# A decoder step's start: bands and first blocks loaded first, the sample later, stores from ScalarE's queue

## The chip, the cores and the metric

The kernel runs on one core of a Trainium2 chip. The metric is the device time of one execution in microseconds, given as the median of the timed runs. TensorE multiplies, VectorE (DVE) and ScalarE (ACT) prepare its operands and take its results, and SyncE (SP) issues nearly all DMA transfers. [...]

## What is computed

One step of a two-layer decoder for 1024 prompt tokens and 64 sample tokens of width 1024, in float32. The change touches only the first mixer, which pools each token's normalised vector over the last 2, 4, 8 or 16 tokens, by group of channels, and the product that the first layer's gate will later need.

```python
# layer 0
u = rmsnorm(h, norm_mix[0])
for g, w in enumerate((2, 4, 8, 16)):            # four groups of 256 channels
    d[g] = (sum of the last w tokens of u[g]) / min(pos + 1, w) - u[g]
h += pool_scale * concat(d[g] @ pool_w[g])       # the sample has 15 earlier tokens in state_pool
h += relu(rmsnorm(h) @ w_up)**2 @ w_down
h += sigmoid(rmsnorm(h) @ w_ple_gate) * (p[0] @ w_ple_proj)
# layer 1 (latent attention, MLP, gate) and the final norm follow
```

## The kernel before

The stream `h` is kept transposed, channels on partitions, in three chunks of tokens (`CH`): chunks 0 and 1 hold 384 prompt tokens each, chunk 2 the last 256 prompt tokens and the 64 of the sample. A product in float32 accuracy is three matmuls on a split into a high and a low part (`mm3`, L188 to L190); the split is a cast on ScalarE (`split`, L146) and a subtraction on VectorE (L147), or the same with a scale (`split_scaled`, L150 and L151).

`pool_phase` is the first stage. The sums over a window are matmuls of a block of 128 tokens (`block_in`: load, sum of squares on ScalarE at L394, reciprocal root in eleven tiny VectorE steps, split into a `slab`) with a banded matrix that `bands` loads and casts (L434, L435). `diff` (L468) makes chunk c, half of its channels, from blocks 3c to 3c+2 and the one before; `diff_sample` (L480) makes the sample's from block 8 (`sample_in`: the sample's own tokens, normalised) and block 9 (`state_in`). `mix` multiplies by `pool_w` and adds to `h`, which `residual` has loaded by then. Until `residual` needs it, the memory of `h` serves as staging for what comes in: `stage(i)` gives place i of eight, 5 to 7 in chunk 0, 0 to 2 in chunk 1, 3 and 4 in chunk 2. There are five slabs and three `raw` tiles.

`proj` is work that nothing here waits for: the product of p[0] with `w_proj` for the gate far behind. 24 of these are spread over the stage to keep TensorE at work; `filler` adds them from the list `fill`. Each needs its chunk's p (`load_p`) and a half of `w_proj` (pieces `proj0_0` and `proj0_1`), is copied out of PSUM into one of three `t` tiles (L366) and stored to DRAM (L367).

The string `order` fixes the order in which this work is written: p loads p of a chunk, f adds so many fillers, b takes a block in (b8 is the sample), s the state, g the bands, d makes sums (chunk, half), S the sample's, m mixes (chunk, half), r loads the residual of a chunk, l writes the last rows. `Plan` loads a weight piece when a step needs it, and ahead of that, up to four pieces, after each step that allows it (`ahead`). What is written is a priority and not a strict order: a later instruction is put earlier on its engine where an earlier one is estimated not to be ready.

Of the kernel before, what the change touches and what calls it, by code (L numbers as in the profile page):

```python
# [24 lines left out]
NS = 64  # L25
T = SEQ + NS
NB = 8
TS = 8
# [3 lines left out]
BUF = 15  # L32
# [80 lines left out]
def kernel(ctx: ExitStack, tc: tile.TileContext, io: dict):  # L113
    nc = tc.nc
# [28 lines left out]
    pp_d = [dpool.tile([KT, P, n], F32, name=f"pp_d{c}") for c, (_, n) in enumerate(CH)]  # L143

    def split(hi, lo, x):
        nc.scalar.copy(out=hi, in_=x)  # L146
        nc.vector.tensor_tensor(out=lo, in0=x, in1=hi.bitcast(F32), op=ALU.subtract)  # L147

    def split_scaled(hi, lo, x, g):
        nc.scalar.activation(hi, x, AF.Copy, scale=g)  # L150
        nc.vector.scalar_tensor_tensor(  # L151
            out=lo, in0=x, scalar=g, in1=hi.bitcast(F32), op0=ALU.mult, op1=ALU.subtract)
# [27 lines left out]
    plan = Plan(load_piece)  # L180

    def raw_tile():
        return wpool.tile([P, 1024], F32, tag="raw", bufs=3, name="raw")
# [8 lines left out]
    S = {}  # L192
# [17 lines left out]
    def bank():  # L210
        return S["ps"].tile([P, 512], F32, tag="mm", bufs=8, name="mm")
# [7 lines left out]
    def slab():  # L219
        return S["hid"].tile([P, 2176], F32R, tag="hid", bufs=5, name="hid")  # L220

    def tmp(n):
        return S["tmp"].tile([P, 384], F32, tag="t", bufs=3, name="t")[:, :n]
# [4 lines left out]
    def tiny(tag, like):  # L228
        p, m = like
        return S["tmp"].tile([P, 10], F32, tag=tag, bufs=4, name=tag)[:p, :m]  # L230

    def rsqrt(v):

        y, t = tiny("y", v.shape), tiny("yt", v.shape)
        nc.vector.tensor_scalar(
            out=y.bitcast(I32), in0=v.bitcast(I32), scalar1=-0.5, scalar2=RSQRT_GUESS, op0=ALU.mult, op1=ALU.add)
        for _ in range(3):
            nc.vector.tensor_tensor(out=t, in0=y, in1=y, op=ALU.mult)
            nc.vector.scalar_tensor_tensor(out=t, in0=t, scalar=-0.5, in1=v, op0=ALU.mult, op1=ALU.mult)
            nc.vector.scalar_tensor_tensor(out=y, in0=t, scalar=1.5, in1=y, op0=ALU.add, op1=ALU.mult)  # L240
        return y
# [35 lines left out]
    def mean_eps(ss, dim):  # L277
        nc.vector.tensor_scalar(out=ss, in0=ss, scalar1=1.0 / dim, scalar2=EPS, op0=ALU.mult, op1=ALU.add)
        return ss
# [38 lines left out]
    def lin(c, w, k, m, mo, src=None):  # L318
        n = CH[c][1]
        wh, wl = (x.rearrange("p (k m) -> p k m", k=k) for x in w)  # L320
        ps = bank()[:, :n]
        x = src or U[c]
        mm3(ps, [(wh[:, i, mo:mo + m], wl[:, i, mo:mo + m], x[i][0], x[i][1]) for i in range(k)])
        return ps

    def four(w, nt):

        return [x[:, 256 * (nt % 4):256 * (nt % 4) + 256] for x in w]
# [5 lines left out]
    def pool_phase():  # L334
# [7 lines left out]
        blocks = {}  # L342
        WAIT, PAIRS = [], ((1, 2), (5, 4), (7, 6))

        pj = [plan.piece(f"proj0_{i}", io["w_proj"][0, i], parts=2 - i) for i in range(2)]
# [16 lines left out]
        def proj(nt, c, w):  # L362
            n = CH[c][1]
            ps = lin(c, four(w, nt), 2, P, 0, PP[c])
            t = tmp(n)
            nc.scalar.copy(out=t, in_=ps)  # L366
            nc.sync.dma_start(out=pp_d[c][nt], in_=t)  # L367

        def start():
            linear_open("1")  # L370
# [8 lines left out]
        def stage(i):  # L379

            c, i = (1, i) if i < 3 else (2, i - 3) if i < 5 else (0, i - 5)
            return h[c].rearrange("p k n -> p (k n)")[:, i * 1024:(i + 1) * 1024]

        def block_in(j):


            if not WAIT:
                E["bss"] = tiny("bss", (P, 2 if any(j == p[0] for p in PAIRS) else 1))
            i = len(WAIT)
            s = slab()  # L390
            blocks[j] = (s[:, 0:1024], s[:, 1024:2048])
            x = stage((3, 4, 0, 1, 2, 0, 3, 4)[j])
            nc.sync.dma_start(out=x, in_=io["x_prompt"][j * P:(j + 1) * P, :])
            nc.scalar.activation(blocks[j][0], x, AF.Square, accum_out=E["bss"][:, i:i + 1])  # L394
            WAIT.append((j, x))
            if any(j == p[0] for p in PAIRS):
                return
            g = rsqrt(mean_eps(E["bss"], D))
            for i, (j, x) in enumerate(WAIT):
                split_scaled(*blocks[j], x, g[:, i:i + 1])  # L400
                if j == 7:
                    E["g7"] = S["tmp"].tile([P, 1], F32, tag="g7", bufs=1, name="g7")
                    nc.vector.tensor_copy(out=E["g7"], in_=g[:, i:i + 1])
            WAIT.clear()

        def sample_in():
            ss = tiny("bss", (NS, 1))
            x, gb = stage(2)[0:NS], stage(7)[0:NS]
            nc.sync.dma_start(out=x, in_=io["x_sample"])
            nc.sync.dma_start(out=gb, in_=io["g_mix0"].partition_broadcast(NS))  # L410
            sq = raw_tile()[0:NS]
            nc.scalar.activation(sq, x, AF.Square, accum_out=ss)
            g = rsqrt(mean_eps(ss, D))
            nc.vector.scalar_tensor_tensor(out=x, in0=x, scalar=g, in1=gb, op0=ALU.mult, op1=ALU.mult)
            blocks[8] = x
            nc.sync.dma_start(out=io["pool_new"], in_=x)

        def last_rows():
            x, gb = raw_tile()[96:P], raw_tile()[96:P]
            nc.sync.dma_start(out=x, in_=io["x_prompt"][SEQ - 32:SEQ, :])  # L420
            nc.sync.dma_start(out=gb, in_=io["g_mix0"].partition_broadcast(32))
            nc.vector.scalar_tensor_tensor(out=x, in0=x, scalar=E["g7"][96:P], in1=gb, op0=ALU.mult, op1=ALU.mult)
            nc.sync.dma_start(out=io["pool_prompt"], in_=x[32 - BUF:32, :])

        def state_in():
            blocks[9] = stage(1)[0:NB * BUF]
            nc.sync.dma_start(out=blocks[9], in_=io["state"].rearrange("b t d -> (b t) d"))
            nc.sync.dma_start(out=io["pool_old"], in_=io["state"][:, TS:BUF, :])

        def bands():  # L430
            s = slab()
# [5 lines left out]
        def d_tile(c, dt):  # L437
            if (c, dt) not in E:
                E[c, dt] = u_pair(c)
            return E[c, dt]  # L440
# [30 lines left out]

        def diff_sample(x):
            xh = x[0].bitcast(F32).rearrange("p (g n) -> p g n", g=4)
            for dt in range(KT):
                g = dt // 2
                cs = slice(dt * P, (dt + 1) * P)
                ps = bank()[:, :NS]
                for bj, o in ((8, 16), (9, 16 + NS)):
                    b = blocks[bj]
                    nc.tensor.matmul(  # L480
                        out=ps, lhsT=b[:, cs], rhs=xh[0:b.shape[0], g, o:o + NS], start=bj == 8, stop=bj == 9)
                uh, ul = d_tile(2, dt)
                split(uh[:, 256:320], ul[:, 256:320], ps)

        def mix(c, gp, w):
# [3 lines left out]
            for gg in range(2):  # L489
# [8 lines left out]
                        op0=ALU.mult, op1=ALU.add)  # L498
                    touch(c, dt)

        fill = [(half, c, nt) for half, c in ((0, 2), (1, 2), (0, 0), (0, 1), (1, 0), (1, 1))
                for nt in range(4 * half, 4 * half + 4)]

        def filler(k):
            for half, c, nt in fill[:k]:
                plan.add(lambda w, nt=nt, c=c: proj(nt, c, w), pj[half])
            del fill[:k]

        def diffs(c, half):
# [2 lines left out]
        def mixes(c, gp):  # L512
# [2 lines left out]
                next_norm(c, gain("norm_mlp0"))  # L515

        order = (
            "p2 f1 b8 f3 b0 s f2 g p0 b1 f2 S b2 f1 b3 f2 p1 b5 d00 f2 d01 f2 b4 r0 "
            "b7 f1 r1 f1 m00 m01 f1 d10 d11 f2 b6 f1 m10 m11 f1 d20 f4 r2 d21 f1 m20 f1 m21 l").split()
        plan.add(start, ahead=False)  # L520
        for i, t in enumerate(order):
            k, a = t[0], int(t[1:] or 0)
            ah = i > 2
            if k == "p":
                plan.add(lambda a=a: load_p(a), ahead=ah)
            elif k == "l":
                plan.add(last_rows)
            elif k == "s":
                plan.add(state_in, ahead=ah)
            elif k == "b":  # L530
                plan.add(sample_in if a == 8 else lambda a=a: block_in(a), ahead=ah)
            elif k == "g":
                plan.add(bands, ahead=ah)
            elif k == "S":
                plan.add(diff_sample, gx)
            elif k == "f":
                filler(a)
            elif k == "d":
                diffs(a // 10, a % 10)
            elif k == "m":  # L540
                mixes(a // 10, a % 10)
            elif k == "r":
                plan.add(lambda a=a: residual(a))
# [875 lines left out]
```

## Time and profile before

| | us |
|---|---|
| median of 3 runs | 2416.49 |
| lowest and highest run | 2413.78, 2417.46 |
| the profiled execution, its own time | 2413.58 |
| its span in the trace | 2411.8 |
| TensorE busy in the span | 2361.0 (98%) |
| VectorE busy | 1226.1 (51%) |
| ScalarE busy | 829.4 (34%) |

The span is the time from the first to the last instruction that the profiler saw; the execution's own time is 1.8 us longer. Busy shares are means over a kernel whose stages differ, so the share of 98% says only that TensorE is the engine to look at, and where it isn't busy is read from the stretches.

### The profile page before, as it was taken

The page shows a single profiled execution, that of the slowest core. Times are in us where ns is not written, and L with a number is a line of the kernel's source. Part 1 is how long each engine was busy: PE and PEld are TensorE (multiplying, and loading weights), DVE is VectorE, ACT ScalarE, POOL GpSimd, SP SyncE. Part 2 cuts the span into 40 slices and gives each one's busy share as a digit, 9 for nine tenths or more (in the row PEclk, how much of TensorE's full clock was granted, in tenths as well). Part 3 has the DMA queues.
Part 4 walks back from the last instruction along what each step waited for, and adds up shares of the span by engine and source line. Part 5 has one row for each costly group of instructions (what it writes and reads, how often), then busy time and mean ns, then how long its engine had stood idle before and what let it go on. Part 6 is the DMA issues. An engine that isn't in the chain of part 4 may idle for free.

```text
span 2411.8 us, 35848 instructions
## 1 busy us (share of the span) xinstructions
PE 2361.0 (98%) x14516; PEld 2308.6 (96%) x14516; DVE 1226.1 (51%) x2406; ACT 829.4 (34%) x1557; POOL 11.0 (0%) x16
## 2 busy tenths in 40 slices
PE   7999999999999999998999999999999999999996
PEld 7999999999999999987988899999999999999996
DVE  5933333333333578477887765433333333334755
ACT  6622121121221444236777644312212212123432
POOL 0000000000000000000000000000000000000001
PEclk8999999999999999999999999999999999999998
DMA  8411111111111143257443351111111111111202
GB/s 269 125 55 44 44 45 44 44 44 47 49 47 44 40 124 130 58 153 223 149 126 125 94 200 55 52 47 49 44 44 44 44 44 44 44 44 44 64 27 78
DMA packets 97085, 186.53 MB, mean 77 GB/s; under 512 B 18633, under 2 KB 69001, under 8 KB 96144
## 3 DMA queue, kind: packets, MB, share of 16 engines
q1 hardware_dynamic: 90535, 179.78, 23.9%
q10 hardware_dynamic: 6384, 4.47, 0.6%
q8 instruction: 114, 1.87, 0.3%
q14 instruction: 52, 0.42, 0.1%
HBM read 155.00 MB, written 28.85 MB: 76 GB/s over the span
## 4 chain that ended last, share of the span: by engine, by line
PE 89%; DVE 4%; DMA 3%; ACT 2%; issue 1%; SPq 1%; ACTq 0%; DVEq 0%
PE mm L188 27%; PE mm L190 27%; PE mm L189 27%; PE s L891 2%; PE one L941 1%; PE one L1006 1%; PE one L918 1%; DMA craw<-in_cache 1%; PE mm L468 1%; ACT p L899 0%; PE mm L269 0%; DVE mx L898 0%; DVE hid L781 0%; PE one L188 0%; DMA hid<-row 0%
## 5 line engine op out<-in xcount | busy, mean ns | idle before, releaser
L188 PE MATMUL mm<-uh,whi 128*128 128x384 f32 (+1 forms) x2460 | 806.8, 328 | 12.8 <-ACT whi L146 5.9
L190 PE MATMUL mm<-uh,wlo 128*128 128x384 f32 (+1 forms) x2460 | 804.9, 327 | 0.2 <-DVE wlo L147 0.2
L189 PE MATMUL mm<-ul,whi 128*128 128x384 f32 (+1 forms) x2460 | 804.6, 327 | 0.0
L190 PE MATMUL mm<-hid,wlo 128*128 128x384 f32 (+1 forms) x1584 | 517.3, 327 | 0.0
L188 PE MATMUL mm<-hid,whi 128*128 128x384 f32 (+1 forms) x1584 | 517.1, 326 | 0.0
L189 PE MATMUL mm<-hid,whi 128*128 128x384 f32 (+1 forms) x1584 | 516.7, 326 | 0.0
L188 PEld LDWEIGHTS mm<-uh,whi 128*128 128x128 f32 x2460 | 464.0, 189 | 21.7 <-ACT whi L146 6.1
L190 PEld LDWEIGHTS mm<-uh,wlo 128*128 128x128 f32 x2460 | 463.9, 189 | 0.7 <-DVE wlo L147 0.7
L189 PEld LDWEIGHTS mm<-ul,whi 128*128 128x128 f32 x2460 | 464.0, 189 | 0.3 <-DVE ul L147 0.3
L146 ACT CAST whi<-raw 128x1024 fp32r<-128x1024 f32 (+3 forms) x184 | 190.9, 1038 | 753.1 <-PE mm L189 740.3
L314 DVE TENSOR_TENSOR h<-h,mm 128x384 f32<-128x384 f32 (+1 forms) x408 | 216.3, 531 | 422.2 <-PE mm L190 418.3
L188 PEld LDWEIGHTS mm<-hid,whi 128*128 128x128 f32 x1584 | 297.3, 188 | 3.8 <-issue 3.8
L190 PEld LDWEIGHTS mm<-hid,wlo 128*128 128x128 f32 x1584 | 297.3, 188 | 0.0
L189 PEld LDWEIGHTS mm<-hid,whi 128*128 128x128 f32 x1584 | 297.2, 188 | 0.0
L147 DVE TENSOR_TENSOR wlo<-raw,whi 128x1024 fp32r<-128x1024 f32 (+3 forms) x184 | 222.0, 1207 | 78.1 <-ACT whi L146 78.0
L557 DVE SCALAR_TENSOR_TENSOR t<-mm,r 128x384 f32<-128x384 f32 (+1 forms) x192 | 102.6, 535 | 299.4 <-PE mm L190 299.4
L559 ACT ACTIVATE t<-t 128x384 f32<-128x384 f32 (+1 forms) x192 | 97.0, 505 | 390.0 <-DVE t L557 390.0
L147 DVE TENSOR_TENSOR hid<-t,hid 128x384 fp32r<-128x384 f32 (+1 forms) x192 | 102.4, 534 | 140.4 <-ACT hid L146 140.4
L258 ACT ACTIVATE sq<-h 128x384 f32<-128x384 f32 (+1 forms) x126 | 63.2, 505 | 121.4 <-DVE h L314 60.2
L146 ACT CAST hid<-t 128x384 fp32r<-128x384 f32 (+1 forms) x192 | 95.0, 495 | 6.0
L259 DVE TENSOR_TENSOR acc<-acc,sq 128x384 f32<-128x384 f32 (+1 forms) x132 | 71.8, 544 | 42.3 <-ACT sq L258 41.5
L151 DVE SCALAR_TENSOR_TENSOR ul<-h,gains,uh 128x384 fp32r<-128x384 f32 (+1 forms) x96 | 54.0, 592 | 4.3 <-ACT uh L150 4.3
(206 smaller groups left out, 1944.6 us busy)
## 6 DMA issues: line engine op xcount, KB each, us to landing
raw<-in_w_up SPq DMA_DIRECT2D x64, 512.0 KB, 3.4
raw<-in_w_down SPq DMA_DIRECT2D x64, 512.0 KB, 3.5
craw<-in_cache SPq DMA_DIRECT2D x64, 192.0 KB, 2.7
raw<-in_w_gate SPq DMA_DIRECT2D x16, 512.0 KB, 3.5
craw<-in_cache SPq DMA_DIRECT2D x64, 128.0 KB, 2.1
h<-in_x_prompt SPq DMA_DIRECT2D x8, 512.0 KB, 6.7
raw<-qn_d SPq DMA_DIRECT2D x8, 512.0 KB, 3.5
q<-q_d SPq DMA_DIRECT2D x8, 512.0 KB, 4.8
```

What stands on the lines that cost most here:

```text
L146: nc.scalar.copy(out=hi, in_=x)
L147: nc.vector.tensor_tensor(out=lo, in0=x, in1=hi.bitcast(F32), op=ALU.subtract)
L151: nc.vector.scalar_tensor_tensor(out=lo, in0=x, scalar=g, in1=hi.bitcast(F32), op0=ALU.mult, op1=ALU.subtract)
L188: nc.tensor.matmul(out=out, lhsT=wh, rhs=xh, start=i == 0, stop=False)
L189: nc.tensor.matmul(out=out, lhsT=wh, rhs=xl, start=False, stop=False)
L190: nc.tensor.matmul(out=out, lhsT=wl, rhs=xh, start=False, stop=i == last)
L258: nc.scalar.activation(s, x, AF.Square)
L259: (add or nc.vector).tensor_tensor(out=acc, in0=acc, in1=s, op=ALU.add)
L314: nc.vector.tensor_tensor(out=h[c][:, dt, :], in0=h[c][:, dt, :], in1=ps, op=ALU.add)
L557: nc.vector.scalar_tensor_tensor(out=r, in0=ps, scalar=0.0, in1=R[c], op0=ALU.max, op1=ALU.mult)
L559: nc.scalar.activation(r, r, AF.Square)
L891: nc.tensor.matmul(out=st[:, a, :seg], lhsT=l[:, qs], rhs=r[:, ks], start=i == 0, stop=i == 4)
```

## The change

The order of the stage is rewritten: the bands and blocks 0, 1 and 2 come ahead of the sample and its state, and fillers of chunk 0 come ahead of the second half of chunk 2's. Up to the step ahead of `d00`, the eleventh in the list, no weight is loaded ahead. The fillers' stores and the store of the sample's normalised rows (`pool_new`) are issued by ScalarE, the latter from `diff_sample`. Block 3 is staged in place 7 and not in place 1, the sample's gain in a `raw` tile and not in place 7, and the copy of the old state rows (`pool_old`) is issued at the stage's end.

```diff
@@ proj
             nc.scalar.copy(out=t, in_=ps)
-            nc.sync.dma_start(out=pp_d[c][nt], in_=t)
+            nc.scalar.dma_start(out=pp_d[c][nt], in_=t)
@@ block_in
-            x = stage((3, 4, 0, 1, 2, 0, 3, 4)[j])
+            x = stage((3, 4, 0, 7, 2, 0, 3, 4)[j])
@@ sample_in
-            x, gb = stage(2)[0:NS], stage(7)[0:NS]
+            x, gb = stage(2)[0:NS], raw_tile()[0:NS]
...
-            nc.sync.dma_start(out=io["pool_new"], in_=x)
@@ last_rows
             nc.sync.dma_start(out=io["pool_prompt"], in_=x[32 - BUF:32, :])
+            nc.sync.dma_start(out=io["pool_old"], in_=io["state"][:, TS:BUF, :])
@@ state_in
-            nc.sync.dma_start(out=io["pool_old"], in_=io["state"][:, TS:BUF, :])
@@ diff_sample
+            nc.scalar.dma_start(out=io["pool_new"], in_=blocks[8])
@@ pool_phase
-        fill = [(half, c, nt) for half, c in ((0, 2), (1, 2), (0, 0), (0, 1), (1, 0), (1, 1))
+        fill = [(half, c, nt) for half, c in ((0, 2), (0, 0), (1, 2), (1, 0), (0, 1), (1, 1))
                 for nt in range(4 * half, 4 * half + 4)]
-        def filler(k):
+        def filler(k, ahead):
             for half, c, nt in fill[:k]:
-                plan.add(lambda w, nt=nt, c=c: proj(nt, c, w), pj[half])
+                plan.add(lambda w, nt=nt, c=c: proj(nt, c, w), pj[half], ahead=ahead)
...
         order = (
-            "p2 f1 b8 f3 b0 s f2 g p0 b1 f2 S b2 f1 b3 f2 p1 b5 d00 f2 d01 f2 b4 r0 "
-            "b7 f1 r1 f1 m00 m01 f1 d10 d11 f2 b6 f1 m10 m11 f1 d20 f4 r2 d21 f1 m20 f1 m21 l").split()
+            "p2 f1 b0 f1 g p0 f2 b1 f2 b2 f2 d00 f2 b3 d01 f2 b8 s p1 S b5 r0 b4 f4 m00 m01 "
+            "b7 r1 f2 d10 d11 f4 b6 m10 f2 m11 d20 r2 d21 m20 m21 l").split()
...
-            ah = i > 2
+            ah = i > 10
...
-                filler(a)
+                filler(a, ah)
```

## Rows read from the trace of the kernel before

**Rows 1.** Busy time by stretch: stretch, length, busy us of each engine, granted clock, DMA.

```profile
0.00:40.00 40.00, 25.40 (x123) 23.11 (x124) 19.98 (x65) 22.18 (x45) 0.70 (x6) 0.83 0.81 264
40.00:120.00 80.00, 79.61 (x503) 76.70 (x502) 70.83 (x174) 56.79 (x113) 0.00 (x0) 1.00 0.52 165
120.00:600.00 480.00, 480.00 (x2919) 480.00 (x2919) 176.67 (x284) 103.02 (x164) 0.00 (x0) 1.00 0.15 46
```

**Rows 2.** TensorE's waits in the first 140 us: who waited for whom, total, times, longest.

```profile
PE mm L188 <- ACT whi L146: 5.9, 1, 5.9
PE mm L188 <- ACT uh L146: 3.6, 1, 3.6
PE mm L480 <- DVE h L414: 2.7, 1, 2.7
```

**Rows 3.** Timeline of TensorE: start, us, instruction, count, idle time before it.

```profile
15.02 0.31 PE L190 MATMUL mm<-uh,wlo 128*128 128x320 f32 x1
18.04 1.30 PE L480 MATMUL mm<-whi,h 64*128 64x64 f32 x10 [2.72 <-DVE h L414]
19.83 1.11 PE L480 MATMUL mm<-whi,h 64*128 64x64 f32 x4 [0.49 <-ACT t L366]
21.35 4.48 PE L480 MATMUL mm<-whi,h 120*128 120x64 f32 x18 [0.41 <-DMA h<-in_state]
29.45 0.69 PE L188 MATMUL mm<-uh,whi 128*128 128x384 f32 x1 [3.61 <-ACT uh L146]
...
33.50 0.35 PE L188 MATMUL mm<-uh,whi 128*128 128x384 f32 x1
...
34.56 1.55 PE L468 MATMUL mm<-hid 128*128 128x384 f32 x8
```

**Rows 4.** SyncE's waits in the first 140 us.

```profile
SPq L367 <- ACT t L366: 34.1, 15, 6.6
```

**Rows 5.** Timeline of SyncE: when loads that the sums need are issued.

```profile
20.27 0.94 SPq L434 DMA_DIRECT2D h<-in_pband  x2
...
26.81 0.90 SPq L393 DMA_DIRECT2D h<-in_x_prompt  x2
```

**Rows 6.** Chain of waits, first 140 us, in order of time: start, us, what.

```profile
21.25 7.61 DMA raw<-in_pT
```

**Rows 7.** Busy time by stretches of 10 us, columns as in Rows 1.

```profile
0.00:10.00 10.00, 4.11 (x17) 3.89 (x18) 2.33 (x5) 3.86 (x6) 0.70 (x6) 1.00 0.69 195
20.00:30.00 10.00, 5.98 (x23) 5.10 (x23) 5.76 (x22) 3.80 (x13) 0.00 (x0) 0.50 0.97 343
...
60.00:70.00 10.00, 9.98 (x74) 9.88 (x73) 10.00 (x21) 9.15 (x20) 0.00 (x0) 1.00 0.70 270
```

**Rows 8.** Tiles of h up to 60 us: durations in ns (min/median/max), first and last start.

```profile
L394 ACT ACTIVATE hid<-h x6: 1056/1060/1062, 18.3 to 49.8; 128x1024 fp32r<-128x1024 f32 x6
...
L150 ACT ACTIVATE hid<-h,y x6: 1136/1151/1153, 22.2 to 55.2; 128x1024 fp32r<-128x1024 f32 x6
L151 DVE SCALAR_TENSOR_TENSOR hid<-h,y,hid x6: 1275/1284/1285, 23.4 to 56.6; 128x1024 fp32r<-128x1024 f32 x6
```

**Rows 9.** Timeline of VectorE: first and last step of one reciprocal root.

```profile
33.65 0.17 DVE L278 TENSOR_SCALAR bss<-bss 128x2 f32<-128x2 f32 x1 [3.19 <-ACT hid L394]
...
35.63 0.16 DVE L240 SCALAR_TENSOR_TENSOR y<-yt,y 128x2 f32<-128x2 f32 x1
```

**Rows 10.** Tiles of raw up to 60 us: cast and subtraction of a load.

```profile
L146 ACT CAST whi<-raw x7: 617/1035/1052, 5.2 to 56.2; 128x1024 fp32r<-128x1024 f32 x4, 128x512 fp32r<-128x512 f32 x2, 128x576 fp32r<-128x576 f32 x1
L147 DVE TENSOR_TENSOR wlo<-raw,whi x7: 691/1217/1226, 5.9 to 57.8; 128x1024 fp32r<-128x1024 f32 x4, 128x512 fp32r<-128x512 f32 x2, 128x576 fp32r<-128x576 f32 x1
```

**Rows 11.** Tile pp_d up to 60 us: its stores, from issue to landing.

```profile
DMA to landing us min/median/max: 2.1/4.4/6.7
```

**Rows 12.** Lines L944 and L697: transfers that ScalarE issues elsewhere, durations in ns.

```profile
L944 ACTq DMA_DIRECT2D o_d<-ot x32: 326/327/363, 1121.7 to 1407.1; - x32
...
L697 ACTq DMA_DIRECT2D ss<-sq x6: 477/492/857, 1023.2 to 1044.9; - x6
```

## The prediction, made before the changed kernel was run

> **What bounds the kernel now.** I read the busy time by long stretches first. From 120 us on TensorE is busy in all 480 of 480 us, at full clock; from 40 to 120 us it is busy for 79.61 of 80; in the first 40 us for 25.40 [rows 1]. So what is taken out of the first 40 us moves all that follows it forward, and nothing this change touches lies later than about 120 us. The kernel's other idle time, far behind, stays where it is.
>
> The waits of TensorE then say what the missing 14.60 us (40 - 25.40) are. The first 5.9 are the start: the first p and the first half of `w_proj` must land and be split [rows 2]; the change leaves this as it is. That leaves 8.7 us: 2.7 for the sample's normalised rows, 3.6 for the split of chunk 0's p, and the rest in pieces of 1 us and less [rows 2]. Both large waits are waits for loads that SyncE issued late: the load of chunk 0's p goes out at 21.25 and takes 7.61 us [rows 6], the bands go out at 20.27, and two blocks only at 26.81 [rows 5]. SyncE is late because it stands before the fillers' stores: 34.1 us in 15 waits for ScalarE's copies [rows 4].
>
> The waits are not all. [...] The sample's 32 matmuls: the first ten took 1.30 us, 0.13 each; the other 22 took 1.11 + 4.48 = 5.59 instead of 22 x 0.13 = 2.86, so 2.7 us lost [rows 3]. The fillers after 29.45: twelve matmuls up to 33.50, 4.05 us [rows 3]. At full clock 2919 matmuls took 480 us [rows 1], 0.1644 each over a mean of 1088/3 columns, so 0.174 for 384 columns and 0.145 for 320; twelve would take 2.09, so 2.0 us lost. What can be won is 8.7 + 2.7 + 2.0 = **13.4 us**, less what the new order wastes in turn.
>
> **The change, part by part.**
>
> *Removed.* The sample and its state no longer stand ahead of the bands and block 0. Their matmuls come after `d01` amid other work, so at full clock: the 2.7 go. SyncE no longer stands before stores: its 34.1 us of waits [rows 4] go, and the loads of `p2 b0 g p0 b1 b2` go out one behind another. Their places in `h` are all fresh, and of the three `raw` tiles they take two and a half pieces' worth in turn (p, `w_proj`, p), so no load among them waits for a split.
>
> *When the inputs land.* By the shapes in the code, in MB: p of chunk 2 0.33, gains 0.04, the first `w_proj` piece 0.52, block 0 0.52, bands 1.05, p of chunk 0 0.39: 2.85 in all. Blocks 1 and 2 make it 3.90, the extra bands (`pextra`) and the second `w_proj` piece 4.71. The first 10 us moved 195 GB/s, 1.95 MB, and with the queue full it was 343 GB/s from 20 to 30 us [rows 7]. So p of chunk 0 lands near 10 + 0.90/0.343 = 12.6 us. With three stores (0.5 MB) among them block 2 lands near 17.1, and with four (0.66) the second `w_proj` piece near 20.0.
>
> *First gap.* Only chunk 2's first four fillers, 24 matmuls, can run before that. In the trace 48 such end at about 15.17 [rows 3], 9.28 us after the start where 48 x 0.145 = 6.96 would do: 2.3 us are the slow first stretch and a short wait for a half of a piece. So 24 end near 5.9 + 3.5 + 1.9 = 11.3 (with all 2.3, 11.7). Chunk 0's p then needs a cast (0.62, half a piece) and a subtraction (0.69) [rows 10]: usable at 13.2 to 13.9, later where ScalarE is at block 0. I take 13.9: a gap of 2.6, between 1.5 and 4.
>
> *Clock after it.* A gap of that length (2.72 plus 0.15) stood before the trace's fall [rows 3]; so I count one slow stretch, at the 2.0 us that the trace's second one cost. Bounds: none, and two (4).
>
> *Second gap.* Four fillers of chunk 0 (24 x 0.174 = 4.2) at 13.9, plus 2.0, last to 20.1, block 0's part of `d00` 1.55 more [rows 3], to 21.6. Blocks 1 and 2 share one reciprocal root: block 2 at 17.1, sum of squares 1.06 and its read 0.19, to 18.4; the root from 33.65 to 35.79 in the trace, 2.15 [rows 9], to 20.5; then 1.15 on ScalarE and 1.28 on VectorE [rows 8]: block 1 usable at 22.9, block 2 at 24.2. The second `w_proj` piece, at 20.0, needs 1.04 and 1.22 [rows 10], to 22.2 if VectorE is free, and brings 3.5 us of fillers (24 x 0.145) that cover the rest up to block 2. I count 1.3 us of wait, between 0 and 3.
>
> *Moved to ScalarE.* 24 stores at 0.33 (0.49 where the source is one row) [rows 12]: 8 to 12 us of a queue that runs in order. Up to `d00` they hide beside the wait for loads. A copy has to wait until the store three ahead has landed, 4.4 us in the middle and 6.7 at most [rows 11]; three copies per 4.4 + 0.8 us is 1.7 us each, against 0.9 to 1.0 of matmuls per filler, and TensorE has eight PSUM banks to run ahead into. Later, ScalarE has less room (9.15 of 10 us from 60 to 70 [rows 7]). I count 0.5 us, between 0 and 2; its worst is a rival below.
>
> *The rest, at nothing.* Block 3 in place 7 no longer waits for the state's matmuls, but holds the second half of chunk 0's residual until it is split; that half is wanted at the second mix, behind `d01`, the sample (32 x 0.13 = 4.2 us) and four fillers (4.2). If that cover were gone, a 0.8 MB load (2.3 us) would show. Block 4 shares place 2 with the sample's rows and so loads after the sample's matmuls; four fillers, two mixes and two fillers (4.2 + 8.4 + 1.8) lie between these and the sums that want it, against a load of about 4 to 8 us, and about 7 for its square, root and splits. The copy of old state rows leaves the busy start for the stage's end, where SyncE has only weights queued, loaded up to four pieces ahead. The second half of `w_proj`, no longer loaded ahead, is the second gap, already counted.
>
> *Sum.* 2.6 + 2.0 + 1.3 + 0.5 = 6.4 us of new waste against 13.4: **7.0 us gained**. The profiled execution (2413.58, the span 2411.8) would become 2406.6. The median of the runs is 2.9 above that execution, so I predict 2416.5 - 7.0 = **2409.5 us**. The ends of the terms: 1.5 in all (gain 11.9, 2404.6) and 4 + 4 + 3 + 2 = 13 (gain 0.4, 2416.1).
>
> **Rivals.**
>
> *Transfers set the pace.* The inputs come no faster than the 264 GB/s that the first 40 us averaged [rows 1], and not 343. Then p of chunk 0 lands at 13.4 and is usable at 14.7 (gap 3.4), block 2 lands at 19.3 and block 1 is usable at 25.1, while cover ends at 22.4 (gap 2.7); a second gap of that length costs a second slow stretch (4.0 in all), with the 0.5 that is 10.6 of waste, a gain of 2.8: 2413.7 us. For it: the DMA engines are at 0.97 from 20 to 30 us [rows 7], so this start is near their limit. Against it: part of what filled them then (sample, state, copies of both, ahead of the bands) is now behind. [...]
>
> *Slower: ScalarE's queue in the full stretch.* From 40 to 120 us VectorE is busy 70.83 of 80, and all 10 of the 10 us from 60, with ScalarE at 9.15 [rows 1, 7]. VectorE's subtraction waits there for ScalarE's cast, and TensorE for both. If VectorE has no room left, TensorE's early start is given back in full at the mixes (0 gained), and the 12 or so stores issued there, 0.33 to 0.49 each on ScalarE [rows 12], add 4 to 6 us: 2421 us. It decides as soon as TensorE arrives at the mixes earlier than VectorE's work can follow. Against it: the blocks' splits, VectorE's work too, also move forward, and VectorE was idle for half of the first 40 us [rows 1].
>
> *The order isn't taken.* The written order is a priority only; if SyncE's queue still puts the late loads late, the gaps move and stay: 2416 us.
>
> **How the numbers follow.** A measurement of this kernel can tell about 0.2% (4.8 us) from no change. Forecast (gain 4.8 to 11.9) 0.62; transfers set the pace (0 to 4.8) 0.25; order not taken 0.05; slower 0.08. Faster is the first, same the two in the middle. The range must leave out no more than 0.2: from 2404.5, the best end, to 2417, which takes in the transfers' rival and the no-change case and leaves out the slower one.
>
> **What would show it.** Right: in the first 40 us TensorE busy for 31 us or more in place of 25.40, the sample's 32 matmuls in 4 to 5 us, the load of chunk 0's p out by 6 us and landed by 13, no wait of SyncE on a `t` copy, and `d10`'s sums (64 matmuls) starting about 7 us sooner. Wrong: new waits of TensorE on block 1, 2 or p of more than 6 us in all, a low clock beyond 20 us, or TensorE idle between 40 and 120 us by more than 2 us on VectorE or ScalarE.

## The result, and the profile after

The changed kernel is slower. Its median is 2440.79 us (2429.09 to 2444.87, six runs) beside 2415.48 us for the kernel before (2412.60 to 2418.88, six runs): a ratio of 1.0095, 95% interval 1.0083 to 1.0108. Predicted were 2409.5 us and a range of 2404.5 to 2417. The profiled execution took 2439.45 us with a span of 2437.6, so 25.8 us more span than before. The changed kernel's runs lie in two groups, two at 2429 to 2432 us with a mean granted clock of 0.990 and four at 2439 to 2445 with 0.983 to 0.985; the profiled one is of the second.

Busy time by stretch, the lines that answer to [rows 1], and below them four stretches of matmuls at the low clock (stretch, length, busy us of each engine, granted clock, share of the DMA engines, GB/s):

```profile
0.00:40.00 40.00, 28.50 (x141) 27.10 (x142) 19.72 (x60) 22.67 (x40) 0.70 (x6) 0.87 0.86 285
40.00:120.00 80.00, 72.05 (x351) 68.49 (x351) 52.52 (x126) 47.28 (x93) 0.00 (x0) 0.77 0.39 129
120.00:600.00 480.00, 480.00 (x2909) 478.31 (x2908) 187.10 (x323) 111.30 (x185) 0.00 (x0) 1.00 0.16 48
...
29.00:35.00 6.00, 6.00 (x26) 6.00 (x26) 4.22 (x6) 3.10 (x7) 0.00 (x0) 0.50 0.79 260
45.50:55.00 9.50, 9.50 (x32) 8.68 (x32) 2.35 (x6) 3.86 (x10) 0.00 (x0) 0.50 0.65 240
74.50:85.00 10.50, 10.50 (x49) 10.50 (x50) 5.11 (x8) 4.21 (x7) 0.00 (x0) 0.50 0.45 150
...
103.50:114.00 10.50, 10.50 (x49) 10.48 (x50) 9.77 (x19) 6.08 (x13) 0.00 (x0) 0.50 0.54 146
```

The first 40 us did get better: TensorE is busy for 28.50 us instead of 25.40. The loss is behind them, where nothing was to happen: from 40 to 120 us TensorE is idle for 7.95 us instead of 0.39, and the granted clock is 0.77 instead of 1.00. In the four lower lines TensorE is busy without a break and still at 0.50. From 120 us on it is busy throughout in both.

TensorE's waits in the first 140 us (who waited for whom: total, times, longest), against [rows 2]:

```profile
PE mm L188 <- ACT whi L146: 5.9, 1, 5.9
PE mm L467 <- ACT hid L150: 5.7, 3, 3.3
PE mm L467 <- ACT whi L146: 2.6, 1, 2.6
PE mm L188 <- ACT uh L146: 2.3, 1, 2.3
PE mm L480 <- DVE h L414: 1.7, 1, 1.7
```

And where they lie, TensorE's timeline against [rows 3] (line 467 is the sums of `diff`, line 480 the sample's matmuls):

```profile
14.46 1.53 PE L188 MATMUL mm<-uh,whi 128*128 128x384 f32 x4 [2.30 <-ACT uh L146]
...
27.83 1.50 PE L467 MATMUL mm<-whi,hid 128*128 128x16 f32 x8 [2.56 <-ACT whi L146]
...
42.38 7.83 PE L480 MATMUL mm<-whi,h 64*128 64x64 f32 x32 [1.67 <-DVE h L414]
...
74.48 10.41 PE L467 MATMUL mm<-hid 128*128 128x256 f32 x48 [3.32 <-ACT hid L150]
...
103.48 10.51 PE L467 MATMUL mm<-hid 128*128 128x256 f32 x48 [2.24 <-ACT hid L150]
```

Each of these five waits has a stretch at the low clock behind it: in windows of 1 us the granted clock is 0.50 from 15 to 18, 29 to 35, 46 to 55, 73 to 86 and 104 to 117 us. The last two rows cost the most. A merged row names the shape of its first instruction only: of these 48 sums 32 have 256 columns and 16 have 16. With the wait, those of chunk 1 occupy 3.32 + 10.41 = 13.7 us; at a granted clock of 1.00 the same mix takes 5.89 (a10, below).

**Idle or slow.** To keep the two apart, I read the first 140 us of each trace in windows of 1 us. Idle is what the matmuls' busy time leaves of a window; lost to the clock is busy time x (1 - granted clock). The kernels of the experiments are in the same table; they are described below.

| kernel | idle | lost to the clock | sum | span |
|---|---|---|---|---|
| before | 15.0 | 4.7 | 19.7 | 2411.8 |
| after | 19.4 | 22.7 | 42.2 | 2437.6 |
| a1: after, stores back on SyncE | 21.5 | 14.2 | 35.7 | 2429.2 |
| a2: before, stores on ScalarE | 14.1 | 6.7 | 20.8 | 2414.7 |
| a6: after, stores on GpSimd | 18.3 | 9.4 | 27.7 | 2422.0 |
| a7: after, sample in place 3 | 19.4 | 14.7 | 34.1 | 2429.2 |
| a8: before, stores on GpSimd | 17.5 | 7.0 | 24.5 | 2424.0 |
| a9: a6 and a7 together | 14.5 | 6.8 | 21.4 | 2417.0 |
| a10: after, cover ahead of late sums | 19.6 | 15.1 | 34.7 | 2431.2 |
| a11: after, sample's matmuls split | 21.9 | 20.6 | 42.4 | 2436.8 |
| a12: a9, sample covered | 16.2 | 6.8 | 23.1 | 2418.2 |
| a13: a9, p and weights first | 20.3 | 18.8 | 39.2 | 2434.6 |
| a14: before, p earlier | 17.5 | 9.6 | 27.1 | 2423.5 |
| a15: before, p and blocks earlier | 17.0 | 15.0 | 31.9 | 2425.0 |
| a16: before, old rows later | 14.3 | 5.2 | 19.5 | 2416.5 |
| a17: a16, sample and p earlier | 15.0 | 11.0 | 25.9 | 2424.7 |

After against before: 4.4 us more idle, 18.0 us more lost to the clock, 22.5 in all of the 25.8 us by which the span grew. For most kernels the sum accounts for the span to within 5 us; for a8 it misses 7.4, for a17 6.7. The table doesn't hold all of the start: the profile gives the granted clock as 1.00 there, yet the first matmuls of 320 columns take 0.27 us each, 18 of them after and 12 before, where later ones take 0.145. So the first 24 end at 12.16 us instead of 11.31. Part of the rest is a stretch from 1000 to 1200 us, which the change doesn't touch and whose clock differs from run to run (0.99 in the trace of before, 0.98 in that of after).

### The profile page after: what moved, and what is told of

It is laid out like the page before. It is cut to its first block, busy times and chain, and to the rows that moved or that the text cites. A ratio compares the mean times of both kernels' runs of the same rounds, so it can differ in the third digit from the quotient of the medians.

```text
span 2437.6 us, 35819 instructions
## 1 busy us (share of the span) xinstructions
PE 2381.3 (98%) x14516; PEld 2327.7 (95%) x14516; DVE 1227.0 (50%) x2406; ACT 833.2 (34%) x1557; POOL 11.0 (0%) x16
## 4 chain that ended last, share of the span: by engine, by line
PE 88%; DVE 4%; DMA 4%; ACT 2%; issue 1%; SPq 1%; ACTq 0%; DVEq 0%
PE mm L188 26%; PE mm L190 26%; PE mm L189 26%; PE s L891 2%; PE one L941 1%; DMA craw<-in_cache 1%; PE mm L467 1%; PE one L918 1%; PE one L1006 1%; PE mm L269 0%; PE one L1078 0%; DVE hid L781 0%; DMA raw<-qn_d 0%; DMA hid<-row 0%; DVE mx L898 0%
## 5 line engine op out<-in xcount | busy, mean ns | idle before, releaser
L146 ACT CAST whi<-raw 128x1024 fp32r<-128x1024 f32 (+2 forms) x184 | 190.7, 1037 | 751.7 <-PE mm L189 740.5
L147 DVE TENSOR_TENSOR wlo<-raw,whi 128x1024 fp32r<-128x1024 f32 (+2 forms) x184 | 222.0, 1207 | 82.4 <-ACT whi L146 82.1
```

## The experiments

Ratios are to the kernel before on the same chip, with 95% intervals; its medians there were 2416.4 to 2418.5 us.

### Which half of the change costs: a1 and a2

Theories: *late blocks* (the order of the work costs: it makes block 4, and blocks 7 and 6 behind it, late, and a1 stays slow, at 2430 to 2445 us), and *stores* (the fillers' stores on ScalarE's queue cost). a1 is the changed kernel with the stores back on SyncE:

```
-            nc.scalar.dma_start(out=pp_d[c][nt], in_=t)
+            nc.sync.dma_start(out=pp_d[c][nt], in_=t)
```

> The changed kernel, but the fillers' stores are issued by SyncE again; order, places and the rest stay as changed. [...] Rival 'stores' (ScalarE's queue and the stores' landings hold up what TensorE waits for): it falls by more than half of the 25 us, below 2427 us.

Measured: 2431.26 us, 1.0073 (1.0056 to 1.0090). a2 is the kernel before with the opposite edit:

> The kernel before, with one part of the change: the fillers' stores are issued by ScalarE; order and places as before. Late blocks: within 5 us of before, 2411 to 2420 us. Stores: 2425 us or more, with waits of TensorE on ScalarE's casts behind copies that wait for a store.

Measured: 2418.72 us, 1.0016 (1.0006 to 1.0026). Both times are those of *late blocks*: with the stores on SyncE the order costs 0.73 of the 0.95% (a1 waits 6.76 us ahead of chunk 2's sums), and the stores' move is no gain even alone. Why not, a2's timeline of TensorE shows:

```profile
18.88 1.71 PE L480 MATMUL mm<-whi,h 64*128 64x64 f32 x8 [2.62 <-DVE h L414]
21.80 5.48 PE L480 MATMUL mm<-whi,h 64*128 64x64 f32 x20 [1.22 <-ACT t L366]
27.82 1.30 PE L480 MATMUL mm<-whi,h 64*128 64x64 f32 x4 [0.54 <-ACT t L366]
31.06 0.69 PE L188 MATMUL mm<-uh,whi 128*128 128x384 f32 x1 [1.94 <-ACT uh L146]
```

The 3.61 us wait for chunk 0's p [rows 3] fell to 1.94, but TensorE now waits for the fillers' copies, and these wait until an earlier store out of the same three `t` buffers has landed (4.4 us in two waits, up to 60 us). SyncE no longer stood in front of the stores; ScalarE stood behind them.

### What the stores wait for: a6 and a8

In the changed kernel's trace SyncE's loads still wait for the fillers' stores, though these are issued elsewhere (SyncE's waits in the first 140 us):

```profile
SPq L168 <- DMA pp_d<-t: 9.9, 2, 5.5
...
SPq L375 <- DMA pp_d<-t: 9.1, 2, 5.2
...
SPq L410 <- DMA pp_d<-t: 5.4, 1, 5.4
...
SPq L393 <- DMA pp_d<-t: 1.1, 1, 1.1
```

That is 25.5 us of waits on landings, in place of 34.1 on copies [rows 4]. Why a load that SyncE issues waits for the landing of a store that ScalarE issued, these rows don't show. a6 is the changed kernel with the stores issued by GpSimd:

```
-            nc.scalar.dma_start(out=pp_d[c][nt], in_=t)
+            nc.gpsimd.dma_start(out=pp_d[c][nt], in_=t)
```

> The changed kernel, but the fillers' stores are issued by GpSimd, whose queue is empty: neither SyncE's nor ScalarE's queue holds them, and no load on SyncE has to wait for the completion of a store. Late blocks: the gap at the extra bands (2.6 us) shrinks, the later ones at the sums stay, 2430 to 2440 us. Stores: below 2427 us.

Measured: 2424.35 us, 1.0035 (1.0022 to 1.0047); none of SyncE's waits on `pp_d` is left. That is the largest single repair, 0.6%, and this time is that of *stores*: the new order costs 0.73% with the stores on SyncE but 0.35% with them on GpSimd, so neither theory holds alone. The run doesn't tell the end of SyncE's waits on landings from the place that the stores took on ScalarE's queue. And its gain is the clock's: by the table idle time falls only from 19.4 to 18.3 us, the time lost to the clock from 22.7 to 9.4. The wait ahead of chunk 1's sums is still 2.80 us, but the low clock behind it ended within 4 us (0.53 to 0.50 from 65 to 68 us, 1.00 from 69); why it ended sooner isn't shown.

The same edit on the kernel before:

> The kernel before with the fillers' stores issued by GpSimd; order and places as before. If SyncE's waits ahead of stores are what makes the loads late: chunk 0's p and the bands are issued 5 us or more earlier, 4 us or more gained, 2412 us or less. If the transfers themselves set the pace, or the completions that a load has to wait for: within 3 us of before.

Measured: 2423.17 us, 1.0014 (1.0005 to 1.0024), so not faster. Taking the 34.1 us of waits off SyncE gives nothing in the old order. But the loads didn't go out 5 us earlier, so this doesn't show that earlier loads are worth nothing. SyncE now stands before the store of the sample's rows (its wait in the first 140 us, then its timeline):

```profile
SPq L416 <- DVE h L414: 6.8, 1, 6.8
...
18.67 0.51 SPq L416 DMA_DIRECT2D out_pool_new<-h  x1
19.22 1.27 SPq L434 DMA_DIRECT2D h<-in_pband  x2
20.59 0.39 SPq L352 DMA_DIRECT2D raw<-in_pT  x1
```

The bands go out at 19.22 instead of 20.27, chunk 0's p at 20.59 instead of 21.25. The copies wait for landings here too, 8.6 us in two waits.

### Block 4 and the sample's place: a7 and a9

a7 stages the sample's rows in place 3, so that block 4 doesn't have to wait for the sample's matmuls:

```
-            x, gb = stage(2)[0:NS], raw_tile()[0:NS]
+            x, gb = stage(3)[0:NS], raw_tile()[0:NS]
```

> The changed kernel, but the sample is staged in place 3 (block 0's, free early) and not in place 2, so that block 4 doesn't wait for the sample's matmuls. Late blocks: the wait of 3.3 us ahead of chunk 1's sums goes and these run at full clock (5.6 and not 10.4 us for 48 matmuls): 8 us or more gained, 2425 to 2433 us. Stores: no change beyond 3 us.

Measured: 2434.85 us, 1.0090 (1.0073 to 1.0107), beside after's 1.0095: no clear difference. TensorE's timeline:

```profile
66.54 8.47 PE L467 MATMUL mm<-hid 128*128 128x384 f32 x64
93.54 1.21 PE L467 MATMUL mm<-hid 128*128 128x256 f32 x8 [2.88 <-ACT hid L150]
95.70 8.70 PE L467 MATMUL mm<-hid 128*128 128x256 f32 x40 [0.95 <-DVE hid L151]
```

Chunk 1's sums run without a wait and at a granted clock of 1.00, but the wait ahead of chunk 2's sums grew from 2.24 to 2.88 + 0.95 us. By the table this execution is still 8.1 us better than the changed kernel's; it is the shortest of four, 2430.95 us, and the others reach 2441.37. So the trace shows a gain that the ratio, over times so far apart, doesn't confirm. Both repairs together are a9:

> The changed kernel with both repairs: stores issued by GpSimd and the sample staged in place 3. If late blocks and stores are separate causes the gains add: 2415 to 2422 us. If both repairs act on the same gaps: within 3 us of the stores' repair alone, 2421 to 2427 us.

Measured: 2422.10 us, 1.0019 (1.0009 to 1.0028), on the border of the two answers. From 40 to 120 us:

```profile
40.00:120.00 80.00, 76.44 (x449) 72.44 (x449) 65.35 (x168) 53.19 (x108) 6.47 (x12) 0.96 0.46 144
```

So these two repairs take back about four fifths of the loss (0.95% to 0.19%). By the ratios the sample's place adds 0.16% to a6's repair, where alone it showed 0.05.

### Is it the wait or the clock: a10, a11 and a12

Two theories share the same waits: *wait alone* (the loss is the idle time) and *clock* (the slow stretch behind a wait costs more than the wait). a10 puts 18 matmuls of 384 columns, three times six into a bank of PSUM (TensorE's result memory) that nothing reads, ahead of chunk 2's 48 sums, which in the changed kernel took 10.51 us behind a wait of 2.24. That is more work than the wait was long:

```
+            if half == 0 and c == 2:
+                cover(3)
```

> [...] Theory 'clock' (a gap of some 2 us ahead of the sums costs mostly by the clock that falls after it and stays low through the sums): the wait goes, the 48 take about 5.6 us, 5 us or more are gained net, 2430 to 2436 us where the changed kernel has 2441. Rival 'wait alone' (the gap costs its own length): 1 us lost, 2440 to 2443 us.

```profile
104.17 5.89 PE L467 MATMUL mm<-hid 128*128 128x256 f32 x48
111.83 0.41 PE L188 MATMUL mm<-uh,whi 128*128 128x320 f32 x1 [1.77 <-DVE ul L151]
```

The wait is gone and the 48 sums take 5.89 us, at a granted clock of 1.00 from 104 to 110, instead of 10.51. With some 3.1 us of added work (18 x 0.174), and a new wait of 1.77 us behind, the ratio still fell from 1.0095 to 1.0083 (1.0066 to 1.0100; 2437.04 us) and the span by 6.4 us, though this trace is of a10's shortest run. The intervals of the two ratios overlap; the 4.6 us on the same 48 matmuls don't depend on them. *Wait alone* is refuted.

The sample's 32 matmuls took 6.86 to 8.55 us in the changed kernel, a1, a6, a7, a9 and a10, against the 4.2 I had counted. Two theories: their own work brings the clock down (cut into parts they keep full clock, and 5 us or more are gained, 2430 to 2436 us), or the gap ahead of them does. a11 cuts them into four parts (`diff_sample` takes the number of a part), each with a filler behind it:

```
-            "... d01 f2 b8 s p1 S b5 r0 b4 f4 m00 m01 "
+            "... d01 f2 b8 s p1 S0 f1 S1 f1 S2 f1 S3 f1 b5 r0 b4 m00 m01 "
```

> The changed kernel with the sample's 32 matmuls of 64 columns cut into four parts of 8, a filler of 6 matmuls between each two. [...] Rival 'the gap ahead of them does it': the clock falls all the same, within 3 us of 2441.

Measured: 2437.38 us, 1.0077 (1.0060 to 1.0093), between the two answers. The clock fell all the same. Its stretch right behind the first part:

```profile
46.00:63.00 17.00, 17.00 (x55) 14.74 (x54) 3.01 (x9) 6.54 (x16) 0.00 (x0) 0.50 0.49 162
```

TensorE was busy for 17 of 17 us and stayed at 0.50. Here a wait of 1.82 us stood ahead of the first part, so a11 can't tell the wait from the matmuls. a12 can: a9 with four fillers moved ahead of the sample's matmuls, so that nothing waits there.

```
-            "... d01 f2 b8 s p1 S b5 r0 b4 f4 m00 m01 "
+            "... d01 f2 b8 s p1 f4 S b5 r0 b4 m00 m01 "
```

> Changed order with GpSimd's stores and the sample in place 3, and four fillers (24 matmuls of 384 columns, about 4.2 us at full clock) moved from behind the sample's matmuls to right ahead of them, so that the sample's rows are ready when TensorE comes to them. In the run that has the first two repairs TensorE waited 0.92 us there, the sample's 32 matmuls took 6.86 us and the clock was low from about 42.8 to 48.7 us. If the waits bring the clock down: no wait, no fall, the sample's matmuls in about 4.2 us, and 4 to 6 us less than that run (2416 to 2418, beside a kernel before near 2417), unless a wait turns up at the sums that lost the four fillers. If the narrow matmuls themselves bring it down: a fall within or just behind them all the same, some 6 to 7 us for them, and no more than 1 us gained.

TensorE's timeline, and its busy time in four stretches of 1 us:

```profile
42.43 0.34 PE L190 MATMUL mm<-uh,wlo 128*128 128x384 f32 x1
42.70 7.15 PE L480 MATMUL mm<-whi,h 64*128 64x64 f32 x32
```

```profile
44.70:45.70 1.00, 1.00 (x7) 0.80 (x6) 0.00 (x0) 0.00 (x0) 0.82 (x2) 1.00 1.05 384
45.70:46.70 1.00, 1.00 (x7) 0.80 (x7) 0.02 (x1) 0.65 (x4) 0.00 (x0) 1.00 1.06 343
46.70:47.70 1.00, 1.00 (x5) 0.88 (x4) 0.76 (x6) 0.62 (x5) 0.54 (x1) 0.51 0.93 315
47.70:48.70 1.00, 1.00 (x5) 0.77 (x4) 0.19 (x1) 0.05 (x1) 0.00 (x0) 0.50 0.99 406
```

No wait, and yet the clock fell 4 us into the 32 matmuls of 64 columns: the second answer of the expectation. The ratio is 1.0015 (1.0005 to 1.0025; 2421.43 us) beside 1.0019, no clear gain. a13, below, shows it a second time: its 32 matmuls begin at 53.37 with TensorE busy from 51 us on without a break, and the clock is at 1.00 from 54 to 57 and at 0.50 from 57 to 63. So in these two runs the clock falls within the sample's 32 matmuls with no wait right ahead of them; what about them does so isn't settled.

### Can an earlier start gain at all: a13 to a17

a13 is a9 with p of chunk 0 loaded ahead of block 0, the second half of `w_proj` ahead of blocks 1 and 2, and fourteen fillers instead of eight ahead of `d00` (the expectation says sixteen; of `order` the first line is shown):

```
-            "p2 f1 b0 f1 g p0 f2 b1 f2 b2 f2 d00 f2 b3 d01 f2 b8 s p1 S b5 r0 b4 f4 m00 m01 "
+            "p2 f1 p0 f3 b0 f4 g f2 b1 f2 b2 f2 d00 f2 b3 d01 b8 s p1 f2 S b5 r0 b4 f2 m00 m01 "
```

> Stores from GpSimd and the sample in place 3 as before, and a new order of the start: chunk 0's p and the second half of w_proj are loaded ahead of the bands and blocks 1 and 2, all sixteen fillers of chunks 2 and 0 run before d00, and two fillers stand ahead of the sample's matmuls. If the low clock behind the waits was what the changed order lost: no wait of 1 us or more in the first 40 us after the start at 5.9, TensorE busy for 32 to 34 of the first 40 us (25.4 in the kernel before, 29.0 with the two repairs), and a time some 5 us below the kernel before (ratio 0.997 to 0.999). If VectorE or ScalarE has no room behind it, the waits turn up again at the sums of chunks 1 and 2 and the ratio is 1.000 to 1.003.

Measured: 2434.56 us, 1.0070 (1.0058 to 1.0082), far off what I expected. ScalarE's timeline shows why:

```profile
11.11 0.73 ACT L366 COPY t<-mm 128x320 f32<-128x320 f32 x2
16.26 0.43 ACT L366 COPY t<-mm 128x320 f32<-128x320 f32 x1 [4.42 <-DMA pp_d<-t]
17.54 0.48 ACT L366 COPY t<-mm 128x384 f32<-128x384 f32 x1 [0.85 <-DMA pp_d<-t]
...
19.32 1.05 ACT L146 CAST whi<-raw 128x1024 fp32r<-128x1024 f32 x1
```

More fillers early means more copies that wait for a store to land: up to 60 us, 11.0 us in six waits, where a9 has 3.1 in two. The fourth copy waits 4.42 us for a landing, the cast of the weights stands behind it on ScalarE, and TensorE waits 4.87 us for that cast. The later sums then came late too (5.09 us of wait, 10.50 for 48).

Four kernels keep the old place of the sample and the stores on SyncE. a14 moves one load of the kernel before, p of chunk 0, ahead of block 0:

```
-            "p2 f1 b8 f3 b0 s f2 g p0 b1 f2 S b2 f1 b3 f2 p1 b5 d00 f2 d01 f2 b4 r0 "
+            "p2 f1 b8 f3 p0 b0 s f2 g b1 f2 S b2 f1 b3 f2 p1 b5 d00 f2 d01 f2 b4 r0 "
```

> The kernel before with one step moved: p of chunk 0 is loaded ahead of block 0 and the state instead of behind the bands. In the kernel before this load went out at 21.25 us, landed 7.61 later, and TensorE waited 3.61 us for its cast. The sample's matmuls stay in the start, where TensorE waits for loads in any case. If the first part of the change's reason is right (late loads of chunk 0's p cost 3.6 us and a slow stretch): the load goes out near 14 us, the 3.61 us wait is under 1, and the ratio is 0.998 to 0.9995. If the transfers are the limit, each load moved forward delays another by the time of its bytes: the wait turns up at the bands or blocks, and the ratio is 0.9995 to 1.001.

Measured: 1.0026 (1.0015 to 1.0037), worse than either theory had it. The wait for p is gone, and two others stand in its place:

```profile
24.55 3.25 PE L480 MATMUL mm<-whi,h 120*128 120x64 f32 x14 [4.24 <-DMA h<-in_state]
...
40.62 0.80 PE L468 MATMUL mm<-hid 128*128 128x256 f32 x4 [3.13 <-ACT hid L150]
```

a15 moves the blocks and the bands forward as well, and the copy of old state rows to the end of the stage:

```
+            "p2 f1 b8 f3 p0 s b0 g b1 f2 S b2 f3 b3 f2 p1 b5 d00 f2 d01 f2 b4 r0 "
```

> The kernel before with p of chunk 0 moved forward as in the run beside it, and besides block 0, the bands and block 1 ahead of the last four fillers' stores of chunk 2 on SyncE's queue and the copy of old state rows at the stage's end: the change's order of loads, but the sample and the state stay in the start and the stores on SyncE. If what the change lost was the sample in the full stretch, the late blocks and the unhooked stores, and its early loads are sound: TensorE busy for 28 to 31 of the first 40 us (25.4 in the kernel before), no wait of 2 us or more behind 40 us, and a ratio of 0.996 to 0.999. If early loads as such only move the waits: 1.000 or above.

Measured: 1.0027 (1.0016 to 1.0038). It waits 4.48 us ahead of the sample and 2.00 and 1.98 at the sums, and SyncE's waits before stores rise from 34.1 to 50.0 us.

a16 is one more part of the change, run alone: the copy of old state rows moved from `state_in` to `last_rows`:

> The kernel before with one part of the change: the copy of old state rows goes out at the stage's end instead of at 18.49 us in the start. If transfers hold the start: the bands and chunk 0's p, queued behind this copy, land 0.7 to 1.5 us earlier, the 3.61 us wait shrinks by as much, and the ratio is 0.9990 to 0.9998. If the copy lay beside other work: 0.9998 to 1.0005.

Measured: 1.0005 (0.9996 to 1.0014): no difference. The wait for chunk 0's p did shrink, from 3.61 to 2.29 us, but small waits ahead of it grew (0.49 to 0.67, 0.41 to 0.64), and the sum of idle and lost time is the same (19.5 against 19.7). a17 is a16 with the state and p of chunk 0 ahead of block 0:

```
+            "p2 f1 b8 s f3 p0 b0 f2 g b1 f2 S b2 f1 b3 f2 p1 b5 d00 f2 d01 f2 b4 r0 "
```

> The run beside it, and the sample's gain, the state and chunk 0's p loaded ahead of block 0. If late loads hold the start: the 2.72 us wait ahead of the sample's matmuls and the 3.61 us wait on chunk 0's p are both under 1.5, no wait of over 1 us turns up at block 0's or block 1's sums, and the ratio is 0.997 to 0.999. If the bytes hold it: a wait of 2 to 4 us turns up at those sums in place of the two, a second slow stretch with it, and the ratio is 1.000 to 1.003.

Measured: 1.0037 (1.0023 to 1.0051), a little beyond what the theory of the bytes allowed. The same trade: the wait for p is 0.71, that ahead of the sample's matmuls stays at 2.71, and block 1's sums come late instead.

```profile
28.61 1.33 PE L188 MATMUL mm<-uh,whi 128*128 128x384 f32 x3 [0.71 <-ACT uh L146]
...
41.02 1.22 PE L468 MATMUL mm<-hid 128*128 128x256 f32 x4 [3.73 <-ACT hid L150]
```

None of these kernels was faster than the kernel before; the best, a16, can't be told from it.

## Why the prediction was wrong, step by step

*What can be won, 13.4 us.* The reading of the first 40 us holds: idle behind the start 8.7, and the table's 4.7 lost to the clock equals the 2.7 + 2.0 that I read off [rows 3]. In the changed kernel the first 40 us hold 11.5 us of idle time and 5.0 lost, together 16.5 against 19.3. So they gave 2.8 us, not 7.0.

*First gap, 2.6.* Right in size, 2.30, in part by luck: both of its ends came later than I had them. The last filler of chunk 2 ended at 12.16 instead of 11.3, because the slow first stretch lasted longer, and chunk 0's p was usable at 14.46 instead of 13.9. What released it was ScalarE: the cast of p began at 13.91, behind block 0's split that had begun at 12.86. I had named that as what can make it later, and had counted the landing. The transfers were no slower than I took them, 390 GB/s from 6 to 14 us.

*Clock after it, one slow stretch at 2.0.* This is the step that failed, in count and in size. Five stretches came, and they lost 22.7 us: 1.6 before 25 us, 3.4 up to 40, 5.1 around the sample, 5.9 and 6.7 at the sums of chunks 1 and 2. My bounds, none and two, looked only at the gaps of the start, and my price came from one stretch of 384-column fillers that ended within 4 us, the end of a granted clock of 0.50 from 20 to 33 us in the kernel before. The two stretches of sums at 0.50 took 10.41 and 10.51 us with TensorE busy all the time. In a10, without the wait, the same 48 matmuls took 5.89. Four of the five falls came with waits of 2.24 to 3.32 us, while the sample's needs no wait (a12).

The price of such a wait isn't fixed by its length, either. Behind the same wait ahead of chunk 1's sums the 48 took 10.41 us in the changed kernel, and in a11:

```profile
79.38 7.52 PE L467 MATMUL mm<-hid 128*128 128x256 f32 x48 [3.32 <-ACT hid L150]
```

What decides how soon the clock comes back is open.

*Second gap, 1.3.* The blocks came nearly in time (0.18 and 0.59). The gap was the 2.56 us ahead of the extra bands' matmuls, which I had not listed. Their cast stands on ScalarE behind a copy that waits for a store, as the rows of ScalarE show:

```profile
22.92 0.45 ACT L366 COPY t<-mm 128x384 f32<-128x384 f32 x1
26.18 0.48 ACT L366 COPY t<-mm 128x384 f32<-128x384 f32 x1 [2.81 <-DMA pp_d<-t]
...
27.11 2.56 ACT L146 CAST whi<-raw 128x576 fp32r<-128x576 f32 x3 [0.45 <-ACT t L366]
```

In the chain of waits that store goes out at 19.46 and lands 6.64 us later.

*Moved to ScalarE, 0.5.* I counted the stores' issue time and the copies' pace, and let the rest run ahead in PSUM. What I left out is what stands behind a waiting copy on ScalarE: casts and splits that TensorE wants. In the rows above, the copy of 26.18 waited 2.81 us for a store to land, and the casts behind it began only at 27.11. The store of 19.46 took 6.64 us, as long as the slowest before (6.7, [rows 11]); but the median of the stores up to 60 us is 3.2 us in the changed kernel and 4.4 before, so the runs don't show that issuing from ScalarE makes a store land sooner or later. a2 and a8, in which only the stores' issuing engine changes (1.0016 and 1.0014), gain nothing.

*SyncE's 34.1 us of waits go.* They did, and 25.5 us of waits on the landings of stores came in their place. Stores from GpSimd, which end these waits and also free ScalarE's queue, are worth 0.6% in the changed order (a6). The 34.1 was too large a reason for the late loads: it is a sum over 140 us, of which 13.3 lie in the first 40, and a8 without them sent bands and p only 1.05 and 0.66 us earlier.

*The sample's 2.7 go.* Wrong, and for a reason that speaks against this change. I took "amid other work" to mean full clock. The 32 matmuls took 7.83 us against my 4.2, and in a12, with no wait ahead of them, still 7.15. In the kernel before they stand in a stretch in which TensorE waits for loads anyway, so a low clock costs little there; the change moved them to where nothing hides it.

*The rest, at nothing.* Block 4 was priced at "about 7 for its square, root and splits", with fillers and mixes as cover. The cover was there, but so was the work of the mixes on the two engines that block 4 needs. Its load went out at 49.63, behind the sample; its square stands at 65.86 and its split at 72.26, ScalarE's rows:

```profile
65.86 1.04 ACT L394 ACTIVATE hid<-h 128x1024 fp32r<-128x1024 f32 x1
...
71.20 1.06 ACT L394 ACTIVATE hid<-h 128x1024 fp32r<-128x1024 f32 x1 [0.71 <-PE mm L467]
...
72.26 2.17 ACT L150 ACTIVATE hid<-h,y 128x1024 fp32r<-128x1024 f32 x2
```

Before, the last square of the first six blocks began at 49.8 and the last split at 55.2 [rows 8]. Now block 4's root took 5.2 us on a full VectorE (67.03 to 72.20) where an undisturbed one takes 2.15 [rows 9], and the square of the next block, which itself waited for TensorE's sums to free a buffer, held ScalarE until 72.26, as long as the root. A step that I had timed on idle engines was moved into a stretch where they were full, and I had those rows [rows 1, 7] in hand.

*The rivals.* The slower one (2421 us) named the right place, ScalarE and VectorE in the full stretch, and the right point of decision, but as its price the issue time of stores and the 7 us given back. It lacked the clock, which made 18.0 of the 22.5 us, and a chance of 0.08 was too small. "Transfers set the pace" fits what became of the loads in the old order: a14, a15 and a17 moved loads forward and got another wait for each that they removed. Its premise, 264 GB/s, did not hold in the changed kernel, where the first 40 us averaged 285 and blocks 1 and 2 came nearly in time.

*What would show it wrong.* I named "a low clock beyond 20 us, or TensorE idle between 40 and 120 us by more than 2 us on VectorE or ScalarE". Both came, and together; I had not worked out what the second does to the first.

*Open.* What about the sample's matmuls brings the clock down; why the clock comes back sooner behind some waits than behind others; why SyncE's loads waited for landings of stores that ScalarE issued; and why the changed kernel's own runs differ by 10 us and more. The other parts of the change (block 3's place, the sample's gain in a `raw` tile, no weight loaded ahead, `pool_new` stored by ScalarE) were not run alone; a9, which keeps them, stands at 1.0019.

## What to carry to other kernels

Price a wait of TensorE with the slow stretch behind it, not by its length: look up in the trace how long the clock stayed low behind each such wait, and what matmuls stand there, and take a range (here 1.6 to 6.7 us behind waits of 2.2 to 3.3). A piece of work that sits in a stretch where its engine waits anyway costs little, even if it is slow; before moving it, time it on the engines as full as they are at the new place, and ask for each waiting instruction what stands behind it on its queue. And when loads already fill the start, moving one forward moves a wait: a14, a15 and a17 each removed a wait of 3 us and got another.

## What the runs showed of the hardware

The granted clock did not come back from 0.50 under steady work as soon as I had thought: TensorE was busy for 10.50 of 10.50 us with sums of 256 and of 16 columns in the changed kernel, and for 17 of 17 us with matmuls of 384 and of 64 columns in a11, at 0.50 throughout. Around waits of 2.24 and 3.32 us ahead of the sums the clock fell; behind waits of 1.18, 0.70 and 1.67 at the like places of a12 it did not. Length alone doesn't decide: behind the same 1.67 us wait in a6 the clock was at 0.50 from 100 to 102. And within 32 matmuls of 64 columns, with 128-column weights loaded for each, the clock went from 1.00 to 0.50 with TensorE shown as busy for the whole microsecond before and after (a12). At the very start the profile gives 1.00 while matmuls of 320 columns run at 0.27 us each, as they do at 0.50 from 29 to 35 us, against 0.145 later: there the pace is that of the low clock, and the granted clock reads 1.00.
